# A hybrid decoder trunk on one core: the first sums of w2's quarters are queued on VectorE behind the last step of the layer norm ahead of the MLP

## The chip, the core and the metric

The kernel runs on one core of a Trainium2 chip. A core has TensorE (PE, matrix products into PSUM), VectorE (DVE), ScalarE (ACT) and GpSimd (POOL), each with an instruction queue of its own that is issued in order, and SyncE (SP), which here only issues transfers from the chip's main memory. Engines wait for each other by semaphores. The metric is the device time of one execution in microseconds. Three runs of the kernel before took 1161.6, 1162.25 and 1165.01 us; the median is 1162.25 us.

## The reference

Two decoder layers on 512 tokens of width 1024, in float32. Each layer is a token mixer and then an MLP, both with a residual and a layer norm behind them:

```python
for i in range(DEPTH):
    h = mixer_sb_ssm(x, ...) if i % 2 == 0 else mixer_dsa(x, ...)
    x = layer_norm(ALPHA * x + h, ln_mix_g[i], ln_mix_b[i])
    x = layer_norm(ALPHA * x + sq_relu_mlp(x, mlp_w1[i], mlp_w2[i]), ln_ffn_g[i], ln_ffn_b[i])

def sq_relu_mlp(x, w1, w2):
    return jnp.square(jax.nn.relu(x @ w1)) @ w2
```

Layer 0 mixes with stick-breaking attention beside a state-space model, layer 1 with sparse attention. w1 is 1024 x 4096, w2 4096 x 1024. This case is about the seam between mixer and MLP: the norm with `ln_mix`, and the first products with w1 and w2 behind it. It is passed twice, once in each layer.

## The kernel before

**Split products.** TensorE works on pairs: each float32 operand is split into a high part, rounded to a shorter format, and the low rest, and a product is three matmuls, high by high, high by low and low by high (`mm3`, lines 131 to 133; lines 841 to 843 in the mixers' projections; lines 311 to 313 in the products with w2). For a weight, ScalarE makes the high part (line 104, or 298 for quarters of w2) and VectorE or GpSimd the low one (line 105, or 299).

**The mixer's last projection.** `out_block` computes one block of 128 tokens by 512 columns in a PSUM bank and VectorE adds it to x (line 848, or line 846 for the first one). Token blocks are numbered 0 to 3 here.

**The layer norm.** When a token block's columns are complete, `layer_norm` runs: the statistics (`bn_stats`, line 181, and line 182), the variance plus a small constant (line 183), its power of -1/2 on GpSimd (line 184), two passes over the whole block with two inputs from SBUF (line 185 and line 189), then eight transposes on TensorE into two PSUM banks (line 199), whose high part ScalarE writes (line 202) and whose low part VectorE writes (line 203), into `xhi` and `xlo`. The MLP's first products read these.

**The MLP.** `up_raw` makes h in groups: `proj_halves` runs the first four column tiles of w1 for tokens 0 to 255 and then for 256 to 511, so that they can begin before the last norms. `down_chunk` multiplies 1024 rows of w2 with a scheme that saves products by forming sums of quarters: w2's chunk has the quarters b11, b12, b21 and b22, each in two tiles of 128 x 1024. It loads b11 and b12, and the first sum is

```python
b12 = load("b12", 0, 1)
combine(b12, b12, b11, ALU.subtract)
```

that is, `b12 - b11` in two instructions on VectorE (line 293), whose result is needed by the scheme's second product. A chunk is a third of w2's first 3072 rows; the first chunk of each MLP is the one with `r0 == 0`. Its loads can start early, since nothing else holds those buffers.

**What sets the order.** Nothing here is ordered by hand apart from the places that say so: a scheduler simulates the program and gives each engine the instruction that it takes to be ready first. An instruction that depends only on loads can so stand between the norms' steps. `issue_after(ins)` makes every instruction that is written inside its block stand behind `ins` on the engine of `ins`. It sets an order of issue only; there is no wait on `ins`.

Of the kernel before, what the change touches and what calls it, by code (L numbers as in the profile page):

```python
# [8 lines left out]
F32 = mybir.dt.float32  # L9
F32R = mybir.dt.float32r  # L10
AF = mybir.ActivationFunctionType
ALU = mybir.AluOpType
# [23 lines left out]
class Trunk:  # L36
# [135 lines left out]
    def layer_norm(self, t, gb, last):  # L172

        nc = self.nc
        xt = self.x[:, t, :]
        n = 2 if not last or t < NB - 1 else 4
        st = self.lnp.tile([P, n, 6], F32, tag="st", bufs=2, name=self.nm("st"))
        mv = self.lnp.tile([P, 2], F32, tag="mv", bufs=2, name=self.nm("mv"))
        rs = self.lnp.tile([P, 2], F32, tag="rs", bufs=2, name=self.nm("rs"))
        for h in range(n):  # L180
            nc.vector.bn_stats(st[:, h, :], xt[:, h * D // n:(h + 1) * D // n])
        nc.vector.bn_aggr(mv, st)
        nc.vector.tensor_scalar(rs[:, 0:1], mv[:, 1:2], LN_EPS, None, ALU.add)  # L183
        nc.gpsimd.tensor_tensor(rs[:, 1:2], rs[:, 0:1], self.mhalf, ALU.pow)  # L184
        nc.vector.scalar_tensor_tensor(xt, xt, mv[:, 0:1], gb[:, 0, :], ALU.subtract, ALU.mult)
        n = n // 2
        for h in range(n):
            c = slice(h * D // n, (h + 1) * D // n)
            nc.vector.scalar_tensor_tensor(xt[:, c], xt[:, c], rs[:, 1:2], gb[:, 1, c], ALU.mult, ALU.add)
            if last:  # L190
                (nc.scalar if h else nc.sync).dma_start(self.out[t * P:(t + 1) * P, c], xt[:, c])
        if last:
            return
        tok = slice(t * P, (t + 1) * P)
        for h in range(2):
            ps = self.bank("pst")
            for i in range(4):
                k = 4 * h + i
                nc.tensor.transpose(ps[:, i * P:(i + 1) * P], xt[:, k * P:(k + 1) * P], self.ident)
            pv = ps.rearrange("p (k c) -> p k c", c=P)  # L200
            hi = self.xhi[:, 4 * h:4 * h + 4, tok]
            nc.scalar.copy(hi, pv)  # L202
            nc.vector.tensor_tensor(self.xlo[:, 4 * h:4 * h + 4, tok], pv, hi.bitcast(F32), ALU.subtract)  # L203

    def mlp(self, w1, w2, g, b, last):

# [66 lines left out]
    def down_chunk(self, hp, w2, r0, hs, u, touched, last):  # L273

        nc, mm = self.nc, self.nc.tensor.matmul
        vec, act = nc.vector, nc.scalar
        a11, a21 = hs[0][:, :, 0:256], hs[0][:, :, 256:512]
        a12, a22 = hs[1][:, :, 0:256], hs[1][:, :, 256:512]  # L280

        def load(tag, j, n):
            ts = []
            for i in range(2):
                t = hp.tile([P, 1024], F32, tag=tag, bufs=2, name=self.nm(tag)).rearrange("p (k c) -> p k c", c=512)
                r = r0 + j * 512 + i * 256
                nc.sync.dma_start(t, w2[r:r + 256, n * 512:n * 512 + 512].rearrange("(k p) c -> p k c", p=P))
                ts.append(t)
            return ts

        def combine(out, x, y, op):
            for o, p, q in zip(out, x, y):
                vec.tensor_tensor(o, p, q, op)  # L293

        def halves(src, pool, c):
            hi = pool.tile([P, 1024], F32R, tag="whi", bufs=4, name=self.nm("whi")).rearrange("p (k c) -> p k c", c=c)
            lo = pool.tile([P, 1024], F32R, tag="wlo", bufs=4, name=self.nm("wlo")).rearrange("p (k c) -> p k c", c=c)
            act.copy(hi, src)  # L298
            vec.tensor_tensor(lo, src, hi.bitcast(F32), ALU.subtract)  # L299
            return hi, lo  # L300

        def product(a, b):
            pss = [self.psb.tile([P, 512], F32, tag="psb", name=self.nm("psb")) for _ in range(2)]
            ahi, alo = halves(a, self.wp, 256)
            for i in range(2):
                bhi, blo = halves(b[i], hp, 512)
                for t, ps in enumerate(pss):
                    tok = slice(t * P, (t + 1) * P)
                    for k in range(2):
                        lh, ll = ahi[:, 2 * i + k, tok], alo[:, 2 * i + k, tok]  # L310
                        mm(ps, lh, bhi[:, k, :], start=i + k == 0, stop=False)  # L311
                        mm(ps, lh, blo[:, k, :], start=False, stop=False)  # L312
                        mm(ps, ll, bhi[:, k, :], start=False, stop=i + k == 2)  # L313
            return pss

        def add(pss, row, col, op=ALU.add):
            for t, ps in enumerate(pss):
                xs = self.x[:, 2 * row + t, col * 512:col * 512 + 512]
                if (row, col, t) in touched:
                    vec.tensor_tensor(xs, xs, ps, op)  # L320
                else:
                    touched.add((row, col, t))
                    vec.scalar_tensor_tensor(xs, xs, ALPHA, ps, ALU.mult, op)

        def gather(pss):
            for t, ps in enumerate(pss):
                if ("u", t) not in touched:
                    touched.add(("u", t))
                    act.copy(u[:, t, :], ps)
                else:  # L330
                    vec.tensor_tensor(u[:, t, :], u[:, t, :], ps, ALU.add)

        b11 = load("b11", 0, 0)
        ps = product(a11, b11)
        add(ps, 0, 0)
        gather(ps)
        yield
        b12 = load("b12", 0, 1)
        combine(b12, b12, b11, ALU.subtract)
        vec.tensor_tensor(a21, a21, a22, ALU.add)  # L340
        ps = product(a21, b12)
        add(ps, 1, 1)
        add(ps, 0, 1)
        yield
        b22 = load("b22", 1, 1)
        vec.tensor_tensor(a11, a21, a11, ALU.subtract)
        s4 = hp.tile([P, 4, 256], F32, tag="s4", bufs=1, name=self.nm("s4"))
        vec.tensor_tensor(s4, a12, a11, ALU.subtract)
        add(product(s4, b22), 0, 1)
        yield  # L350
        combine(b12, b22, b12, ALU.subtract)
        b21 = load("b21", 1, 0)
        gather(product(a11, b12))
        yield
        vec.tensor_tensor(a11, a22, a11, ALU.subtract)
        combine(b11, b12, b11, ALU.subtract)
        ps = product(a11, b11)
        add(ps, 1, 0)
        add(ps, 1, 1)
        yield  # L360
        combine(b22, b12, b21, ALU.subtract)
        add(product(a12, b21), 0, 0)
        yield
        add(product(a22, b22), 1, 0, ALU.subtract)
        if last:
            for row, col in ((0, 1), (1, 0), (1, 1)):
                xs = self.x[:, 2 * row:2 * row + 2, col * 512:col * 512 + 512]
                vec.tensor_tensor(xs, xs, u, ALU.add)
        yield
# [838 lines left out]
```

## Time and profile before

| what | value |
|---|---|
| median of three runs | 1162.25 us |
| profiled execution, its own time | 1163.17 us |
| its span (first to last instruction) | 1161.4 us |
| mean granted TensorE clock | 0.987 |
| TensorE busy | 1111.9 us, 96% |
| VectorE busy | 840.6 us, 72% |
| ScalarE busy | 532.6 us, 46% |
| GpSimd busy | 172.2 us, 15% |
| line 293, all 48 instructions | 60.3 us on VectorE |

All times in a trace are microseconds from the span's start. A timeline row gives start, duration, engine, line, operation, output <- inputs, the tile's shape and how many equal instructions were merged; in brackets stand the engine's idle time before the row and what ended it. Durations of neighbours on an engine can overlap a little. In tile names numbers are left out, so `b` stands for any quarter of w2, `psb` for a PSUM bank of a projection, `pst` for one of transposes. A row of stretches gives for each stretch its length, the busy time and the instructions of TensorE, its weight loads, VectorE, ScalarE and GpSimd, then the granted clock of TensorE (1.00 is full speed), the share of the transfer engines and GB/s. The chain of waits is the work that ended last, followed back from the end; "issue" in it is time in which an engine waited for nothing that is seen.

The norm ahead of the MLP lies at 229 to 268 us in layer 0 and at 800 to 832 us in layer 1.

### The profile page before, as it was taken

To read this page: it belongs to the slowest core of one execution; us is meant where nothing else is said; L and a number is where in the kernel's file an instruction comes from. 1 tells how busy PE (TensorE), PEld (TensorE's weight loads), DVE (VectorE), ACT (ScalarE), POOL (GpSimd) and SP (SyncE) were. 2 spreads that over 40 slices of the span, in tenths; PEclk is the share of its full clock that TensorE was granted. 3 is DMA by queue.
4 is the path that set the end of the run, shared out by engine and by line. 5 is a ranking of instruction groups with operands and counts; after the bars stand their busy time and mean duration, and the time that the engine had idled before them with its cause. 6 is when DMAs were issued, how large, how long until landed. Compare 5 with 4: busy or idle time off the path is not lost.

```text
span 1161.4 us, 15563 instructions
## 1 busy us (share of the span) xinstructions
PE 1111.9 (96%) x5860; PEld 926.4 (80%) x5860; DVE 840.6 (72%) x1255; ACT 532.6 (46%) x832; POOL 172.2 (15%) x201
## 2 busy tenths in 40 slices
PE   7989999999999999999999979997999999999997
PEld 6878877779888888888898867775988888888886
DVE  7996598694667875965568998557548678587736
ACT  5534386424544444554135446552445445445520
POOL 1043230320000000000121655325000000000001
PEclk9998999999999999999999989998999999999999
DMA  7526683651243252333046860008304415315101
GB/s 246 143 62 157 189 223 96 194 168 39 61 145 101 62 159 73 97 112 87 1 120 158 216 189 1 2 9 264 109 19 127 131 33 152 120 38 162 37 1 73
DMA packets 147307, 126.99 MB, mean 109 GB/s; under 512 B 24353, under 2 KB 115297, under 8 KB 147233
## 3 DMA queue, kind: packets, MB, share of 16 engines
q1 hardware_dynamic: 145552, 123.59, 36.9%
q10 hardware_dynamic: 1680, 2.41, 0.6%
q8 instruction: 46, 0.75, 0.3%
q14 instruction: 29, 0.23, 0.1%
HBM read 105.80 MB, written 5.37 MB: 96 GB/s over the span
## 4 chain that ended last, share of the span: by engine, by line
PE 85%; DVE 6%; DMA 4%; issue 2%; ACT 2%; SPq 1%; POOL 0%; POOLq 0%; DVEq 0%; ACTq 0%
PE psa L131 12%; PE psa L133 12%; PE psa L132 12%; PE psb L311 7%; PE psb L313 7%; PE psb L312 7%; PE pso L949 3%; PE pst L942 3%; PE psb L382 3%; PE psb L381 3%; PE psb L380 3%; PE psl L1142 2%; PE psb L841 2%; PE psb L842 2%; PE psb L843 2%
## 5 line engine op out<-in xcount | busy, mean ns | idle before, releaser
L133 PE MATMUL psa<-xhi,wlo 128*128 128x512 f32 (+1 forms) x720 | 267.0, 371 | 0.0
L132 PE MATMUL psa<-xlo,whi 128*128 128x512 f32 (+1 forms) x720 | 266.5, 371 | 0.0
L131 PE MATMUL psa<-xhi,whi 128*128 128x512 f32 (+1 forms) x720 | 265.6, 371 | 0.2 <-ACT xhi L202 0.2
L104 ACT CAST whi<-raw 128x1024 fp32r<-128x1024 f32 (+1 forms) x129 | 133.6, 1046 | 204.6 <-PE psa L132 126.4
L105 DVE TENSOR_TENSOR wlo<-raw,whi 128x1024 fp32r<-128x1024 f32 (+1 forms) x102 | 128.2, 1260 | 86.9 <-ACT whi L104 85.8
L132 PEld LDWEIGHTS psa<-xlo,whi 128*128 128x128 f32 x720 | 135.7, 188 | 23.3 <-DVE xlo L203 0.4
L133 PEld LDWEIGHTS psa<-xhi,wlo 128*128 128x128 f32 x720 | 135.7, 188 | 23.2
L131 PEld LDWEIGHTS psa<-xhi,whi 128*128 128x128 f32 x720 | 135.0, 188 | 23.1 <-ACT xhi L202 0.5
L299 DVE TENSOR_TENSOR wlo<-b,whi 128x1024 fp32r<-128x1024 f32 x84 | 102.6, 1222 | 42.9 <-ACT whi L298 42.8
L311 PE MATMUL psb<-whi,whi 128*128 128x512 f32 x336 | 130.7, 389 | 0.0
L312 PE MATMUL psb<-wlo,whi 128*128 128x512 f32 x336 | 130.7, 389 | 0.0
L313 PE MATMUL psb<-whi,wlo 128*128 128x512 f32 x336 | 129.7, 389 | 0.0
L298 ACT CAST whi<-b 128x1024 fp32r<-128x1024 f32 x84 | 88.3, 1051 | 41.9 <-PE psb L313 30.2
L105 POOL TENSOR_TENSOR wlo<-raw,whi 128x1024 fp32r<-128x1024 f32 x27 | 69.7, 2591 | 135.6 <-ACT whi L104 134.5
L184 POOL TENSOR_TENSOR rs<-rs,two 128x1 f32<-128x1 f32 x16 | 22.4, 1402 | 424.2 <-DVE rs L183 424.2
L313 PEld LDWEIGHTS psb<-whi,wlo 128*128 128x128 f32 x336 | 63.1, 188 | 13.2
L312 PEld LDWEIGHTS psb<-wlo,whi 128*128 128x128 f32 x336 | 63.1, 188 | 13.1
L311 PEld LDWEIGHTS psb<-whi,whi 128*128 128x128 f32 x336 | 63.1, 188 | 13.0
L293 DVE TENSOR_TENSOR b<-b,b 128x1024 f32<-128x1024 f32 x48 | 60.3, 1262 | 12.3 <-DMA b<-in_w_dram 11.8
L298 ACT CAST whi<-h 128x1024 fp32r<-128x1024 f32 x36 | 38.0, 1054 | 54.0 <-PE psb L312 34.0
L299 DVE TENSOR_TENSOR wlo<-h,whi 128x1024 fp32r<-128x1024 f32 x36 | 44.0, 1222 | 14.2 <-ACT whi L298 13.5
L841 PE MATMUL psb<-whi,xhi 128*128 128x512 f32 x128 | 51.6, 411 | 0.8 <-DVE rs L183 0.6
(263 smaller groups left out, 1967.5 us busy)
## 6 DMA issues: line engine op xcount, KB each, us to landing
raw<-in_w_dram SPq DMA_DIRECT2D x80, 512.0 KB, 4.1
b<-in_w_dram SPq DMA_DIRECT2D x48, 512.0 KB, 4.6
raw<-in_w_in_dram SPq DMA_DIRECT2D x29, 512.0 KB, 4.4
raw<-in_w_out_dram SPq DMA_DIRECT2D x16, 512.0 KB, 4.6
qst<-hl SPq DMA_DIRECT2D x48, 128.0 KB, 3.5
kst<-hl SPq DMA_DIRECT2D x24, 256.0 KB, 4.4
gb<-in_ln_g_dram SPq DMA_DIRECT2D x4, 512.0 KB, 4.0
gb<-in_ln_b_dram SPq DMA_DIRECT2D x4, 512.0 KB, 5.2
```

Source lines behind the costliest of these rows:

```text
L104: nc.scalar.copy(hi[:, c], raw[:, c])
L105: (eng or nc.vector).tensor_tensor(lo[:, c], raw[:, c], hi[:, c].bitcast(F32), ALU.subtract)
L131: mm(ps, lhi, rhi, start=start, stop=False)
L132: mm(ps, lhi, rlo, start=False, stop=False)
L133: mm(ps, llo, rhi, start=False, stop=stop)
L293: vec.tensor_tensor(o, p, q, op)
L298: act.copy(hi, src)
L299: vec.tensor_tensor(lo, src, hi.bitcast(F32), ALU.subtract)
L311: mm(ps, lh, bhi[:, k, :], start=i + k == 0, stop=False)
L312: mm(ps, lh, blo[:, k, :], start=False, stop=False)
L313: mm(ps, ll, bhi[:, k, :], start=False, stop=i + k == 2)
L841: nc.tensor.matmul(ps, chi[:, k, tok], whi, start=i == 0, stop=False)
```

## The change

The last `tensor_tensor` that `layer_norm` writes (line 203, block 3's second half) is kept in `self.normed`, and the first chunk's first sum is written inside `issue_after(self.normed)`:

```diff
@@ layer_norm
-            nc.vector.tensor_tensor(self.xlo[:, 4 * h:4 * h + 4, tok], pv, hi.bitcast(F32), ALU.subtract)
+            last_lo = nc.vector.tensor_tensor(self.xlo[:, 4 * h:4 * h + 4, tok], pv, hi.bitcast(F32), ALU.subtract)
+        self.normed = last_lo.ins
@@ down_chunk
         b12 = load("b12", 0, 1)
-        combine(b12, b12, b11, ALU.subtract)
+        with self.tc.issue_after(self.normed) if r0 == 0 else nullcontext():
+            combine(b12, b12, b11, ALU.subtract)
         vec.tensor_tensor(a21, a21, a22, ALU.add)
```

Two instructions of each layer are so held behind the norm on VectorE; the loads, the other chunks and the arithmetic are the same. In the changed file lines move down by one from line 204 and by two from line 341: line 293 becomes 294, 299 becomes 300, 846 and 848 become 848 and 850.

Since the scheduler simulates the whole program, other instructions near the two places change their order too. On VectorE in layer 0, before (`x<-x,psb` adds a projection's half block; `psb_2262` is block 1's first half, `rs_2320` block 0's factor, `rs_2372` block 1's):

```order
L181 BN_STATS st_2318<-x 128x6
L293 TENSOR_TENSOR b_488_2898<-b_488_2898,b_472_2817 128x1024
L182 BN_AGGR mv_2319<-st_2318 128x2
L293 TENSOR_TENSOR b_489_2900<-b_489_2900,b_473_2819 128x1024
L848 TENSOR_TENSOR x<-x,psb_2262 128x512
L183 TENSOR_SCALAR rs_2320<-mv_2319 128x1
L185 SCALAR_TENSOR_TENSOR x<-x,mv_2319,gb_1311 128x1024
```

And now:

```order
L182 BN_AGGR mv_2319<-st_2318 128x2
L183 TENSOR_SCALAR rs_2320<-mv_2319 128x1
L185 SCALAR_TENSOR_TENSOR x<-x,mv_2319,gb_1311 128x1024
L850 TENSOR_TENSOR x<-x,psb_2262 128x512
L189 SCALAR_TENSOR_TENSOR x<-x,rs_2320,gb_1311 128x1024
L181 BN_STATS st_2370<-x 128x6
L850 TENSOR_TENSOR x<-x,psb_2276 128x512
L181 BN_STATS st_2370<-x 128x6
L182 BN_AGGR mv_2371<-st_2370 128x2
L183 TENSOR_SCALAR rs_2372<-mv_2371 128x1
L185 SCALAR_TENSOR_TENSOR x<-x,mv_2371,gb_1311 128x1024
L850 TENSOR_TENSOR x<-x,psb_2290 128x512
```

Block 0's steps now follow each other, and the sums stand 40 instructions later, between the last line 203 and the first line 300:

```order
L203 TENSOR_TENSOR xlo<-pst_2435,xhi 128x4x128
L294 TENSOR_TENSOR b_488_2898<-b_488_2898,b_472_2817 128x1024
L294 TENSOR_TENSOR b_489_2900<-b_489_2900,b_473_2819 128x1024
L300 TENSOR_TENSOR wlo_2828<-b_472_2817,whi_2827 128x1024
L300 TENSOR_TENSOR wlo_2844<-b_473_2819,whi_2843 128x1024
```

On TensorE in layer 0, block 0's transposes (`pst_2328`, `pst_2335`) stood behind both halves of block 2's projection, together with block 1's; now they stand between these halves, and block 1's first four behind the second half. Block 1's second four move behind the first matmul of the MLP, and block 2's eight stand together behind the first half of the MLP's matmuls for tokens 0 to 255; this half reads only what block 1's first four deliver, or `xhi`. In layer 1 TensorE's order is as it was. There VectorE had, before (`psb_7111`, `psb_7137` and `psb_7163` are blocks 0, 1 and 2):

```order
L293 TENSOR_TENSOR b_1367_7761<-b_1367_7761,b_1351_7680 128x1024
L293 TENSOR_TENSOR b_1368_7763<-b_1368_7763,b_1352_7682 128x1024
L846 SCALAR_TENSOR_TENSOR x<-x,psb_7111 128x512
L846 SCALAR_TENSOR_TENSOR x<-x,psb_7137 128x512
L181 BN_STATS st_7189<-x 128x6
L181 BN_STATS st_7239<-x 128x6
L846 SCALAR_TENSOR_TENSOR x<-x,psb_7163 128x512
```

And now, up to block 0's line 189:

```order
L848 SCALAR_TENSOR_TENSOR x<-x,psb_7111 128x512
L181 BN_STATS st_7189<-x 128x6
L848 SCALAR_TENSOR_TENSOR x<-x,psb_7137 128x512
L182 BN_AGGR mv_7190<-st_7189 128x2
L181 BN_STATS st_7239<-x 128x6
L848 SCALAR_TENSOR_TENSOR x<-x,psb_7163 128x512
L183 TENSOR_SCALAR rs_7191<-mv_7190 128x1
L185 SCALAR_TENSOR_TENSOR x<-x,mv_7190,gb_7084 128x1024
L181 BN_STATS st_7263<-x 128x6
L182 BN_AGGR mv_7240<-st_7239 128x2
L181 BN_STATS st_7263<-x 128x6
L189 SCALAR_TENSOR_TENSOR x<-x,rs_7191,gb_7084 128x1024
```

Block 0's line 189 now stands ahead of block 1's lines 183 and 185, and the two sums stand behind the last line 203 here too.

## The prediction, as put on record before the run

> **What bounds the kernel now.** I read the page first (share of the chain that ended last by engine), then TensorE's rows with an idle time, then the same stretches in the chain of waits and in VectorE's timeline.
>
> The page's part 4:
>
> ```profile
> PE 85%; DVE 6%; DMA 4%; issue 2%; ACT 2%; SPq 1%; POOL 0%; POOLq 0%; DVEq 0%; ACTq 0%
> ```
>
> TensorE is the path for 85% of 1161.4 us. An edit of VectorE's order pays only where TensorE waits for VectorE. TensorE's timeline around the two layer norms ahead of an MLP (start, duration, line; idle time before, releaser in brackets):
>
> ```profile
> 236.63 0.50 PE L841 MATMUL psb<-whi,xhi 128*128 128x512 f32 x1 [0.64 <-DVE rs L183]
> 245.23 1.23 PE L199 MATMUL pst<-ident,x 128*128 128x128 f32 x8 [1.99 <-DVE x L189]
> 265.59 1.03 PE L199 MATMUL pst<-ident,x 128*128 128x128 f32 x8
> ...
> 798.34 0.39 PE L843 MATMUL psb<-whi,xlo 128*128 128x512 f32 x1
> 800.61 0.39 PE L843 MATMUL psb<-whi,xlo 128*128 128x512 f32 x1
> 809.26 1.97 PE L199 MATMUL pst<-ident,x 128*128 128x128 f32 x8 [8.26 <-DVE x L189]
> 819.65 0.38 PE L132 MATMUL psa<-xlo,whi 128*128 128x256 f32 x1
> ```
>
> Layer 0 has two waits there (0.64 and 1.99 us), layer 1 one of 8.26 us, each for VectorE. The granted clock around layer 0's second wait (view by stretches; the number before the DMA share is the clock):
>
> ```profile
> 242.00:245.20 3.20, 1.25 (x10) 0.92 (x8) 3.20 (x6) 1.07 (x2) 1.53 (x1) 1.00 0.00 0
> 245.20:249.30 4.10, 4.07 (x16) 3.39 (x17) 4.07 (x8) 1.40 (x3) 0.69 (x1) 0.60 0.00 0
> 249.30:253.20 3.90, 3.90 (x18) 3.25 (x17) 3.43 (x5) 2.91 (x3) 0.77 (x1) 0.98 0.11 27
> ```
>
> After it the clock is 0.60 for 4.10 us, so 4.10 x 0.40 = 1.64 us more are lost. That the moved sums (line 293) stand in what TensorE waits for, the chain of waits shows:
>
> ```profile
> 231.92 1.30 DVE b L293
> 233.22 1.48 issue
> 234.69 0.20 DVE mv L182
> 234.89 1.09 DVE b L293
> ...
> 790.00 7.66 DMA b<-in_w_dram
> 797.78 1.30 DVE b L293
> 799.28 1.21 DVE b L293
> 800.50 1.19 DVE x L846 x2
> ```
>
> In layer 1 the chain even runs over the load of the quarter that the sum needs. VectorE's timeline:
>
> ```profile
> 231.92 2.85 DVE L293 TENSOR_TENSOR b<-b,b 128x1024 f32<-128x1024 f32 x1
> 234.81 1.17 DVE L293 TENSOR_TENSOR b<-b,b 128x1024 f32<-128x1024 f32 x1
> 236.56 1.27 DVE L185 SCALAR_TENSOR_TENSOR x<-x,mv,gb 128x1024 f32<-128x1024 f32 x1
> 243.90 1.28 DVE L189 SCALAR_TENSOR_TENSOR x<-x,rs,gb 128x1024 f32<-128x1024 f32 x1
> 272.96 1.22 DVE L299 TENSOR_TENSOR wlo<-b,whi 128x1024 fp32r<-128x1024 f32 x1 [4.83 <-ACT whi L298]
> ...
> 797.78 2.72 DVE L293 TENSOR_TENSOR b<-b,b 128x1024 f32<-128x1024 f32 x2 [1.76 <-DMA b<-in_w_dram]
> 800.42 1.27 DVE L846 SCALAR_TENSOR_TENSOR x<-x,psb 128x512 f32<-128x512 f32 x2
> 814.46 3.95 DVE L105 TENSOR_TENSOR wlo<-raw,whi 128x1024 fp32r<-128x1024 f32 x3 [0.17 <-ACT whi L104]
> 818.92 1.28 DVE L203 TENSOR_TENSOR xlo<-pst,xhi 128x512 fp32r<-128x512 f32 x2
> 836.34 1.23 DVE L299 TENSOR_TENSOR wlo<-b,whi 128x1024 fp32r<-128x1024 f32 x1 [4.93 <-ACT whi L298]
> ```
>
> The sums hold VectorE 2.85 + 1.17 = 4.02 us in layer 0 and 2.72 us in layer 1 (after 1.76 us of waiting). At the place they move to, behind the last line 203 and ahead of the first line 299, VectorE sits idle for 4.83 and 4.93 us.
>
> **The change part by part.** Nothing is added or removed: four sums, two in each layer, change their place on VectorE; no DMA moves, and SyncE's and GpSimd's orders are the same. In layer 0 TensorE's order and one cast of ScalarE change too.
>
> *Layer 0.* With the sums gone, token block 0's norm starts at 231.92, where the first sum started. Its mean (line 182) and line 183 end by about 232.2; the two-input pass of line 185 comes next. GpSimd is still splitting weights then:
>
> ```profile
> 225.49 8.20 POOL L105 TENSOR_TENSOR wlo<-raw,whi 128x1024 fp32r<-128x1024 f32 x3 [0.87 <-ACT whi L104]
> 236.72 1.53 POOL L184 TENSOR_TENSOR rs<-rs,two 128x1 f32<-128x1 f32 x1 [3.03 <-DVE rs L183]
> ```
>
> It ends at 233.69, and the sum that ran beside it took 2.85 us, its sister 1.17. So line 185 costs between 1.27 and 2.85 us; I take the slow end, because GpSimd's work lies under it: done by about 234.9. Line 184 cannot start before 233.7 and takes 1.53, so line 189 has its factor at 235.3. Behind line 185 stands line 848 for block 1's first half (0.6 us: the two of line 846 at 800.42 take 1.27), done by 235.5. It frees the PSUM bank that TensorE waited for until 236.63; the matmuls before that wait ended at 236.63 - 0.64 = 235.99. **The 0.64 us go.** Line 189 then ends at about 236.7.
>
> TensorE now runs block 2's first half of the projection (12 matmuls of 0.227 us: from 798.34 to 800.61 there are ten) from about 235.8 to 238.55 and then block 0's transposes, which the new order puts there: ready since 236.7. Block 2's second half fills 239.6 to 242.3, and the transposes of block 1 follow. They need the second line 189, which before ended at 243.90 + 1.28 = 245.18. From 236.7 VectorE has ahead of it lines 181, 848, 181, 182, 183, 185, 848 and 189, 0.6 + 0.6 + 0.6 + 0.2 + 0.1 + 1.2 + 0.6 + 1.2 = 5.1 us, so 241.8. **TensorE arrives at 242.3: the 1.99 us go**, with 0.5 us to spare, and I let the slow clock of 1.64 us go with the gap. Layer 0: 0.64 + 1.99 + 1.64 = **4.3 us**. As a check I count what TensorE issues from 235.8 to the transposes of block 3 without a wait: 48 matmuls of the projection x 0.227, 96 of the MLP's first half x 0.12 (six in 0.72 us below), six fours of transposes x 0.5 (1.03 us for eight), 10.9 + 11.5 + 3.0 = 25.4: 261.2 in place of 265.59, 4.4 us. Block 3's line 189 follows block 2's transposes by a cast, a split, lines 182 to 185 and line 184 on GpSimd, and I put it at 260.6, some 0.5 us before.
>
> ```profile
> 820.11 0.28 PE L132 MATMUL psa<-xlo,whi 128*128 128x256 f32 x1
> ...
> 820.83 0.28 PE L132 MATMUL psa<-xlo,whi 128*128 128x256 f32 x1
> ```
>
> *Layer 1.* Here the sums waited for their load. The matmul at 798.34 ends block 0's projection (0.39 later, 798.73); VectorE can take line 846 at 798.77 and not at 800.42: **1.65 us**. From there to the splits of block 1 (818.92) VectorE runs the same set of instructions in both orders, with one wait of 0.17 us in 18.5, so the splits come 1.65 to 1.8 us earlier; I take **1.7**. Line 189 of block 0 rises over other blocks' passes: from 798.77 it has 7.0 us of passes to its end (seven of 0.6, two means, line 183, two of 1.2), 805.8 in place of 809.1. TensorE's 8.26 us shrink by 3.3 to about 5; but at 819.65 it needs block 1's splits, which three weight splits (3.95 us) hold up, and there it waits out the difference, about 1.6 us. Bounds: 1.65 (VectorE all the way) and 3.3 (if TensorE alone counted).
>
> *At the new place* the sums cost 2 x 1.2 = 2.4 us, in idle times of 4.83 and 4.93. Queued behind them is line 299 of the unsummed quarter, which waits for ScalarE anyway. The summed quarter's cast comes later:
>
> ```profile
> 276.08 1.05 ACT L298 CAST whi<-b 128x1024 fp32r<-128x1024 f32 x1 [0.17 <-issue]
> ```
>
> With everything 4.3 us earlier it comes at 271.8, the first sum ends near 265: nothing is late. Without that cover it would be 2.4 us in each layer.
>
> **Sum:** 4.3 + 1.7 = 6.0 us. Behind both places TensorE is busy (no idle time over 0.4 us from 270 to 600 and from 810 on), and weight loads start when buffers come free, so the gain should be kept. The profiled execution took 1163.17 (1.8 around its span): 1157.2. It lies 0.9 above the median of 1162.25, from which it would be 1156.2. I say **1157**.
>
> [...] The row first: a gap of 1.99 us was followed by a clock of 0.60. [...]
>
> ```profile
> 611.66 0.59 PE L1084 MATMUL psx<-kist,qist 96*128 96x256 f32 x3 [1.76 <-issue]
> 611.60:616.00 4.40, 4.34 (x35) 4.21 (x36) 2.80 (x6) 1.97 (x7) 0.00 (x0) 1.00 1.06 268
> ```
>
> [...]
>
> **The rivals.** (1) *The slow clock stays.* The gap goes, but the work from 245 on meets a clock of 0.60 for 4.1 us all the same. For it: 1.76 us did not slow TensorE at 611.66. Against: the slow stretch begins with the first transposes behind the gap. Gain 4.4: 1158.8.
>
> (2) *The wait moves on.* My spare time in layer 0 is 0.5 us at blocks 1 and 3. If VectorE's chain comes 2 us late at one of them, TensorE waits there, and the clock falls again: 4.3 - 2.0 - 1.6 = 0.7, with layer 1's 1.7 a gain of 2.4: 1160.8. For it: GpSimd's overlap, and a queue now packed with norm passes. Against: 5.1 us of passes counted row by row.
>
> (3) *Nothing arrives.* A load behind these places sets the pace, and both gains are waited out there: 1163.2. For it: in layer 1 the chain ran through a load of w2. Against: DMA is 4% of the chain, and that load leaves it.
>
> (4) *Slower: the sums hold up the MLP.* They go from a stretch in which TensorE still waits for other things to the head of the products. If the cast at 276.08 waited for them and the norms gained nothing, 2 x 2.4 = 4.8 us: 1168.0. It decides once the sums end later than that cast could start, over 6 us later than I have them. Against: the idle 4.83 and 4.93 us.
>
> **How the numbers follow.** Forecast 0.60, rivals 0.11, 0.11, 0.11 and 0.07. A measurement of this kernel can tell about 0.3%, 3.5 us, from no change. The forecast is faster by that, the first rival nearly always; (2) and (3) are within it: faster 0.70, same 0.23, slower 0.07. The range: below, layer 1's bound of 3.3 with the lower median, 1162.25 - 7.6 = 1154.6, and a us for runs; above, the second rival with its scatter: 1153.5 to 1161.5. Left out are most of (3) and (4).
>
> **What would show it.** In the changed trace: no idle time of TensorE over 0.4 us and a clock of 1.00 from 236 to 253; the transposes of block 3 near 261.1; line 846 near 798.8; TensorE's gap in layer 1 near 5 us and a second one of 1 to 2 us ahead of the first line 132; line 294 inside VectorE's idle time ahead of line 300. Wrong would be: a gap at the transposes of block 1 or 3 of layer 0, or a time above 1159.

## The result and the profile after

| what | before | changed kernel |
|---|---|---|
| median of six runs | 1164.26 us (1161.6 to 1165.01) | 1156.85 us (1155.07 to 1158.38) |
| ratio of the times, 95% interval | | 0.9946 (0.9934 to 0.9959) |
| profiled execution, its own time | 1163.17 us | 1157.72 us |
| its span | 1161.4 us | 1155.9 us |

The change makes the kernel 0.54% faster, between 0.41 and 0.66%. The two medians lie 7.4 us or 0.64% apart, still inside that interval. Forecast were 1157 us and a gain of 6.0 us; the gain is 5.45 us between the two profiled executions and, by the ratio, 6.3 us. Of the page's shares of the chain that ended last, this is the row by engine; TensorE's share was 85% before, the transfers' (DMA) 4%:

```profile
PE 86%; DVE 7%; DMA 3%; issue 2%; ACT 1%; SPq 1%; POOL 0%; POOLq 0%; DVEq 0%; ACTq 0%
```

TensorE's timeline of the changed kernel around the two norms (lines of the changed file, so 199 is as before, 843 to 845 are the projection's products):

```profile
239.41 1.04 PE L199 MATMUL pst<-ident,x 128*128 128x128 f32 x8
243.04 0.60 PE L199 MATMUL pst<-ident,x 128*128 128x128 f32 x4
261.79 1.04 PE L199 MATMUL pst<-ident,x 128*128 128x128 f32 x8
...
802.87 1.97 PE L199 MATMUL pst<-ident,x 128*128 128x128 f32 x8 [4.86 <-DVE rs L183]
813.64 0.66 PE L199 MATMUL pst<-ident,x 128*128 128x128 f32 x4 [0.33 <-DVE x L848]
814.24 0.39 PE L132 MATMUL psa<-xlo,whi 128*128 128x256 f32 x1
```

In layer 0 no transpose waits any more. In layer 1 the long wait is 4.86 us instead of 8.26. (The view names line 183 as what ended it; block 0's line 189, which these transposes read, ended beside it, at 802.81.) The view by stretches says the same of layer 0 (length; busy time of TensorE, its weight loads, VectorE, ScalarE, GpSimd; granted clock): TensorE is busy for all of 26 us and its clock is 1.00 throughout.

```profile
236.00:262.00 26.00, 26.00 (x174) 23.82 (x173) 24.29 (x35) 7.55 (x10) 4.47 (x4) 1.00 0.48 146
```

VectorE's timeline of the changed kernel at the places that the prediction costed:

```profile
229.83 0.68 DVE L850 TENSOR_TENSOR x<-x,psb 128x512 f32<-128x512 f32 x1
233.19 2.42 DVE L185 SCALAR_TENSOR_TENSOR x<-x,mv,gb 128x1024 f32<-128x1024 f32 x1
236.14 1.27 DVE L189 SCALAR_TENSOR_TENSOR x<-x,rs,gb 128x1024 f32<-128x1024 f32 x1
241.47 1.28 DVE L189 SCALAR_TENSOR_TENSOR x<-x,rs,gb 128x1024 f32<-128x1024 f32 x1
259.97 1.28 DVE L189 SCALAR_TENSOR_TENSOR x<-x,rs,gb 128x1024 f32<-128x1024 f32 x1 [0.44 <-POOL rs L184]
264.25 2.35 DVE L294 TENSOR_TENSOR b<-b,b 128x1024 f32<-128x1024 f32 x2
269.18 1.23 DVE L300 TENSOR_TENSOR wlo<-b,whi 128x1024 fp32r<-128x1024 f32 x1 [2.58 <-ACT whi L299]
...
795.78 0.69 DVE L848 SCALAR_TENSOR_TENSOR x<-x,psb 128x512 f32<-128x512 f32 x1 [2.49 <-PE psb L845]
809.49 3.49 DVE L105 TENSOR_TENSOR wlo<-raw,whi 128x1024 fp32r<-128x1024 f32 x3
813.50 1.88 DVE L203 TENSOR_TENSOR xlo<-pst,xhi 128x512 fp32r<-128x512 f32 x3
825.91 2.35 DVE L294 TENSOR_TENSOR b<-b,b 128x1024 f32<-128x1024 f32 x2
830.92 1.23 DVE L300 TENSOR_TENSOR wlo<-b,whi 128x1024 fp32r<-128x1024 f32 x1 [2.65 <-ACT whi L299]
```

The sums stand in what was idle time: ahead of the first line 300 VectorE is now idle for 2.58 and 2.65 us, and before for 4.83 and 4.93. Within 0.1 us that is the sums' 2.35 us: they took up idle time.

**Where the 5.5 us of span come from.** I cut both executions at the same five places. The first is the start of the first add of the projection (before: the row below; after: 229.83). The second is the transposes of block 3 in layer 0 (265.59, 261.79). The third is the end of TensorE's work ahead of its long wait in layer 1 (809.26 - 8.26 = 801.00; 802.87 - 4.86 = 798.01). The fourth is the first line 132 of layer 1 (819.65, 814.24). The last is the end. The row of the kernel before, from VectorE's timeline:

```profile
228.99 0.67 DVE L848 TENSOR_TENSOR x<-x,psb 128x512 f32<-128x512 f32 x1
```

| stretch | before | after | difference |
|---|---|---|---|
| start to the first add | 228.99 | 229.83 | +0.84 |
| to the transposes of block 3, layer 0 | 36.60 | 31.96 | -4.64 |
| to the long wait of layer 1 | 535.41 | 536.22 | +0.81 |
| to the first line 132 of layer 1 | 18.65 | 16.23 | -2.42 |
| to the end | 341.75 | 341.66 | -0.09 |

The two norms gave 4.64 and 2.42 us, 7.06 together. 1.65 us of it were lost in stretches that the edit doesn't touch. Of the first loss (0.84 us), 0.54 us are there within the first 12 us: a matmul that starts at 11.35 us before starts at 11.89 us now. Of the second (0.81 us), 0.69 us come with the clock. TensorE's timeline shows the attention's products of layer 1 behind a long wait that both kernels have (of the same length, though the view names another end for it); of the kernel before:

```profile
692.35 5.57 PE L1142 MATMUL psl<-kst,qst 128*128 128x384 f32 x24 [7.11 <-DVE pst L1149]
```

and of the changed kernel:

```profile
688.68 6.26 PE L1144 MATMUL psl<-kst,qst 128*128 128x384 f32 x24 [7.10 <-DMA qst<-hl]
```

They are the same 24 products, and they take 0.69 us longer. The granted clock from their start on was 0.66 over 6.3 us before and 0.55 over 6.4 us after. Why that differs between two executions of equal work, no run here shows; the last section comes back to it.

### The profile page after: what moved, and what is told of

Its sections match the earlier page's. It is cut to its first block, busy times and chain, and to the rows that moved or that the text cites. A ratio compares the mean times of both kernels' runs of the same rounds, so it can differ in the third digit from the quotient of the medians.

```text
span 1155.9 us, 15562 instructions
## 1 busy us (share of the span) xinstructions
PE 1113.2 (96%) x5860; PEld 928.3 (80%) x5860; DVE 839.0 (73%) x1255; ACT 532.8 (46%) x832; POOL 172.4 (15%) x201
## 4 chain that ended last, share of the span: by engine, by line
PE 86%; DVE 7%; DMA 3%; issue 2%; ACT 1%; SPq 1%; POOL 0%; POOLq 0%; DVEq 0%; ACTq 0%
PE psa L132 12%; PE psa L133 12%; PE psa L131 12%; PE psb L313 7%; PE psb L314 7%; PE psb L312 7%; PE pso L951 3%; PE pst L944 3%; PE psb L383 3%; PE psb L382 3%; PE psb L384 3%; PE psb L843 2%; PE psl L1144 2%; PE psb L844 2%; PE psb L845 2%
```

## The experiments

Each edit is made to the changed kernel, and each median stands beside runs of the kernel before on the same chip.

**One layer at a time.** The sums are held in layer 0 alone:

```diff
-        with self.tc.issue_after(self.normed) if r0 == 0 else nullcontext():
+        with self.tc.issue_after(self.normed) if r0 == 0 and self.n_mlp == 1 else nullcontext():
```

> Only layer 0's first sums are held behind the norm; layer 1 stays as before. My theory (VectorE's passes ahead of the transposes are the price, and the slow clock goes with the gap): 4.3 to 4.7 us under the kernel before, ratio about 0.996; no idle time of TensorE over 0.4 us and a clock of 1.00 at 236 to 262 us of the span, layer 1's gap 8 us as before. Rival (the slow clock is not the gap's and stays): 2.6 to 3 us under before, with a clock near 0.6 for some 4 us near 245.

Measured: 1160.5 us against 1164.43, ratio 0.9964 (0.9952 to 0.9976), so 4.2 us less. Its TensorE has no idle time from 236 to 253 us and a clock of 1.00; in layer 1 its wait is like that of the kernel before:

```profile
236.00:253.00 17.00, 17.00 (x99) 14.84 (x98) 16.86 (x26) 6.47 (x8) 2.98 (x2) 1.00 0.44 143
...
806.61 1.97 PE L199 MATMUL pst<-ident,x 128*128 128x128 f32 x8 [8.46 <-DVE x L189]
```

In layer 1 alone (`self.n_mlp == 2` in the same place):

> Only layer 1's first sums are held; layer 0 stays as before. My theory: 1.7 to 2.4 us under the kernel before, ratio 0.998 to 0.9985: the gap shrinks from 8.3 to about 4.9 us, but VectorE's splits of block 1 set the pace behind it. Layer 0 shows its gap of 2 us and the slow clock behind it once more; the two single changes add up to the whole, 6 to 7 us. Rival (TensorE's gap counts in full): 3.4 us under before, ratio 0.997.

Measured: 1161.01 us against 1164.43, ratio 0.9971 (0.9962 to 0.9981), so 3.4 us less, with an interval of 2.2 to 4.4. The interval takes in my 2.4 and the rival's 3.4. From its trace:

```profile
246.18 1.09 PE L199 MATMUL pst<-ident,x 128*128 128x128 f32 x8 [1.97 <-DVE x L189]
...
806.75 1.97 PE L199 MATMUL pst<-ident,x 128*128 128x128 f32 x8 [4.85 <-DVE x L189]
818.12 0.38 PE L132 MATMUL psa<-xlo,whi 128*128 128x256 f32 x1
```

From the end of the projection (806.75 - 4.85 = 801.90) to the first line 132 it takes 16.22 us, 2.4 less than before (18.65) and 3.0 less than with layer 0 alone (there from 806.61 - 8.46 = 798.15 to 817.40: 19.25). So layer 1 is worth 2.4 to 3.0 us. In this execution layer 0's wait of 1.97 us was there, but the eight transposes behind it took 1.09 us and not 1.23, and the granted clock over the 4.1 us from them on was 1.00: no slow clock followed it. The two layers' ratios take 0.36 and 0.29% off, 0.65 together; the whole change takes 0.54% (0.41 to 0.66). Within that noise they add up.

**How much room the new place has.** The held sums are undone and made again once (so six sums stand where two would do), and then three times:

```diff
             combine(b12, b12, b11, ALU.subtract)
+            for _ in range(1 if r0 == 0 else 0):
+                combine(b12, b12, b11, ALU.add)
+                combine(b12, b12, b11, ALU.subtract)
```

> The change, with the held sum made three times in each layer's first chunk (b12 - b11, + b11, - b11; the result is the same but for rounding): 4 more instructions of 1.2 us in each layer at the new place. My theory: they fill VectorE's idle time there (2.6 us up to the first line 300, then 0.2, 1.5 and more) and end before the summed quarter's cast, so the time stays within 1 us of the changed kernel, ratio to before about 0.994. Rival (the sums hold up the MLP's products): 4.8 us in each layer more, 9.6 in all, ratio about 1.002.

Measured: 1156.9 us, ratio 0.9939 (0.9925 to 0.9952): no cost, as expected.

> The change, with the held sum made seven times: 12 more instructions, 14 us in each layer, at the new place. They end some 9 us behind the place where the summed quarter's cast stands in the changed kernel, and the splits of the unsummed quarter are late too. My theory: here the cover is gone; each layer loses something between 2 and 9 us, the time lies 4 to 18 us above the changed kernel. Rival (nothing waits for VectorE there, since the first products come much later): within 1.5 us of the changed kernel.

Measured: 1156.16 us, ratio 0.9936 (0.9923 to 0.9949). Twelve sums more, some 14 us of VectorE in each layer, cost nothing, and my expectation of 4 to 18 us fell. VectorE's and ScalarE's rows of that run:

```profile
263.69 5.76 DVE L294 TENSOR_TENSOR b<-b,b 128x1024 f32<-128x1024 f32 x5
273.91 6.89 DVE L294 TENSOR_TENSOR b<-b,b 128x1024 f32<-128x1024 f32 x6
283.38 1.06 ACT L299 CAST whi<-b 128x1024 fp32r<-128x1024 f32 x1 [0.39 <-DVE b L294]
297.64 1.23 DVE L345 TENSOR_TENSOR h<-h,h 128x1024 f32<-128x1024 f32 x1 [6.27 <-ACT h L229]
```

The scheduler laid line 300's splits between the sums and moved the summed quarter's cast back; that cast waits 0.39 us for a sum, and VectorE still idles for 6.27 us ahead of 297.64. So the cover at the new place isn't the 4.8 us of one idle time but the idle times of VectorE behind it taken together. The fourth rival's price (2.4 us a layer, from a delay of 6 us on) has no place here: 14 us didn't reach it.

**One sum held, one left free.**

```diff
-            combine(b12, b12, b11, ALU.subtract)
+            combine(b12[:1], b12[:1], b11[:1], ALU.subtract)
+        combine(b12[1:], b12[1:], b11[1:], ALU.subtract)
```

> The change with only the first of the two sums held behind the norm in each layer; the second is free, and the scheduler puts it behind block 0's line 185 in layer 0 and ahead of block 0's projection sum in layer 1, and TensorE's order in layer 0 differs from the change's. Theory (each sum of 1.2 us on VectorE ahead of the transposes counts about once, less the spare time of 0.5 us and the wait for the load): 1 to 2.5 us above the changed kernel, ratio to before 0.995 to 0.997. Rival (only the first sum, the one of 2.85 us beside GpSimd, was the cost): within 0.7 us of the changed kernel.

Measured: 1164.84 us against 1165.02, ratio 1.000 (0.9991 to 1.001). Nothing is left of the gain; my theory and its rival both had some. TensorE and VectorE:

```profile
253.37 0.58 PE L132 MATMUL psa<-xlo,whi 128*128 128x256 f32 x1 [2.62 <-DVE xlo L203]
...
801.43 1.22 DVE L294 TENSOR_TENSOR b<-b,b 128x1024 f32<-128x1024 f32 x1 [2.62 <-DMA b<-in_w_dram]
...
811.42 1.97 PE L199 MATMUL pst<-ident,x 128*128 128x128 f32 x8 [7.86 <-DVE x L189]
```

In layer 1 the reason is plain: the free sum still waits for its load in front of the norm, so VectorE stands for 2.62 us, and TensorE waits 7.86. In layer 0 block 1's transposes went behind block 3's projection in TensorE's order, and the wait moved on to the first line 132: 2.62 us, and a clock of 0.50 from 253.37 up to 259.1. That is the prediction's second rival, seen in a neighbour of the change. One free sum, with the other order that the scheduler then gave both engines, was enough for it. So the runs show what the held sums and the new order do together; none of them shows what the 4.02 us of VectorE's time alone would have given in layer 0.

**Is TensorE short of cover in layer 1?** I let the scheduler write each norm of layer 1 three blocks behind its projection and not two, so that another projection stands in front of block 0's transposes:

```diff
-                                   for t in range(NB)], gb, False)
+                                   for t in range(NB)], gb, False, 3)
```

> The change, and in layer 1's mixer the norms follow three blocks behind the projection and not two, so that TensorE has block 3's 24 matmuls (5.4 us) in the gap of 4.9 us that the change leaves there. VectorE's order keeps the three weight splits of line 105 ahead of block 1's splits. Theory (VectorE is the bound of layer 1's seam): the gap closes and opens again at the first lines 199 or 132, the time stays within 1 us of the changed kernel, ratio about 0.994. Rival (TensorE's gap and the slow clock behind it are the cost): 4 to 6 us under the changed kernel, ratio about 0.990.

Measured: 1160.64 us against 1164.26, ratio 0.9969 (0.9958 to 0.9981). That is 2.7 us more than the changed kernel by the ratios, whose intervals just touch (0.9958 and 0.9959); I had expected a change of a us at most, the rival a gain. Both were wrong about the time. Its TensorE:

```profile
802.83 1.09 PE L199 MATMUL pst<-ident,x 128*128 128x128 f32 x8 [0.55 <-DVE rs L183]
808.81 1.97 PE L199 MATMUL pst<-ident,x 128*128 128x128 f32 x8 [4.90 <-DVE x L189]
813.59 0.39 PE L132 MATMUL psa<-xlo,whi 128*128 128x256 f32 x1 [1.77 <-DVE xlo L203]
```

The wait of 4.9 us closes at block 0 (0.55) and opens again at block 1 (4.90). VectorE had, between block 0's line 189 and block 1's, two weight splits that depend on a load and its cast alone (of its timeline):

```profile
804.55 1.21 DVE L105 TENSOR_TENSOR wlo<-raw,whi 128x1024 fp32r<-128x1024 f32 x1
805.79 1.17 DVE L105 TENSOR_TENSOR wlo<-raw,whi 128x1024 fp32r<-128x1024 f32 x1
807.48 1.28 DVE L189 SCALAR_TENSOR_TENSOR x<-x,rs,gb 128x1024 f32<-128x1024 f32 x1
```

It is the sums' fault again with other instructions. So the splits alone were held behind block 1's norm:

```diff
@@ layer_norm
+        if t == 1:
+            self.normed_1 = last_lo.ins
@@ up_raw
-                        ps = self.proj_fm(w1, (c * 8 + f) * P, None)
+                        with self.tc.issue_after(self.normed_1) if first and self.n_mlp == 2 else nullcontext():
+                            ps = self.proj_fm(w1, (c * 8 + f) * P, None)
```

> The change, and in layer 1 the low parts of w1's next four column tiles (line 105) are queued behind block 1's last split on VectorE. Theory: VectorE's chain to block 1's splits is 3.5 us shorter, but TensorE, still with its gap of 4.9 us and the slow clock, arrives only 0.3 to 0.6 us before the splits of the changed kernel: 0.3 to 1 us under the changed kernel, ratio about 0.9938. Rival (VectorE alone is the bound): 3.5 us under it, ratio 0.9915.

Measured: 1158.13 us, ratio 0.9948 (0.9935 to 0.996), as the changed kernel; the rival's 3.5 us fall, and the 0.3 to 1 us of my theory can't be told from nothing. TensorE still waits for block 0's norm, and VectorE then waits for TensorE, where the splits stood:

```profile
803.47 1.82 PE L199 MATMUL pst<-ident,x 128*128 128x128 f32 x8 [4.85 <-DVE rs L183]
...
811.71 0.69 DVE L851 SCALAR_TENSOR_TENSOR x<-x,psb 128x512 f32<-128x512 f32 x1 [1.53 <-PE psb L848]
```

Then both edits together:

> Both edits of the two runs before. Theory (each of two chains of about the same length sets the pace, so only both together pay): 2.5 to 4.5 us under the changed kernel, ratio 0.990 to 0.992, with 1 to 3 us of waiting left ahead of block 1's transposes or first line 132. Rival (a third thing sets the pace, such as the power on GpSimd or the casts): within 1 us of the changed kernel.

Measured: 1154.47 us (1152.79 to 1155.91), ratio 0.9916 (0.9902 to 0.9931), as expected: faster than both kernels, by 3.5 us against the change by the ratios, and the intervals do not touch. TensorE's waits there are 2.25 and 1.58 us, and eight transposes take 1.09 us, at a granted clock of 1.00 (801.29 to 811.52):

```profile
805.62 1.09 PE L199 MATMUL pst<-ident,x 128*128 128x128 f32 x8 [2.25 <-DVE x L189]
809.26 0.39 PE L132 MATMUL psa<-xlo,whi 128*128 128x256 f32 x1 [1.58 <-DVE xlo L203]
```

Either edit alone gives nothing or costs; the later norms need a VectorE that is free for them, and the free VectorE needs work of TensorE that comes first.

**Three more executions** were to show whether the slow clock behind layer 0's wait is a rule. The kernel before, twice, and layer 1 alone, once more:

> The kernel before, profiled once more. The gap of 2.0 us in layer 0 left a clock of 0.60 for 4.1 us in the first profile and a clock of 1.00 in the run with layer 1's change alone. If the slow clock follows such a gap by chance, this profile shows either; if the first was the rule it shows 0.6 again. The time is 1161 to 1167 us.

> The kernel before, profiled a third time, for the clock behind layer 0's gap of 2.0 us. So far 0.60, 0.65 and, with layer 1's change, 1.00 over the 4.1 us from the transposes on. If it is chance, either may show; if layer 1's change made the difference, it is near 0.6 again.

> Layer 1's change alone, profiled again, for the same clock. Chance: either 1.00 or about 0.6. If layer 0 of this kernel differed in something, 1.00 again, though its order there is that of the kernel before.

They took 1163.47, 1167.35 and 1162.34 us, one execution each. All three had the wait ahead of layer 0's transposes (1.97, 1.99 and 1.95 us) and a slow clock behind it (0.64, 0.67 and 0.61 over 4.1 us). The last section sets them beside the execution without it.

## Why the prediction was right, point by point

- **Layer 0: 4.3 us forecast, 4.64 measured** (4.2 by the runs with layer 0 alone). All three terms went: the 0.64 us at the PSUM bank, the 1.99 us at the transposes, and the slow clock, for which the clock of 1.00 over 26 us stands. Block 3's transposes come 31.96 us behind the first add; I had put them at 261.1 to 261.2, and without the 0.84 us by which this execution came later to the norm they are at 260.95.
- **Its working held in detail.** Line 185 beside GpSimd (three weight splits there, 226.32 to 234.53) took 2.42 us (bounds 1.27 and 2.85, taken 2.85). Without the 0.84 us, block 0's line 189 ends at 236.57 (237.41 in the row; 236.7 forecast), the second one at 241.9 (242.75; 241.8 forecast), and TensorE's transposes for it begin at 242.2 (243.04; 242.3 forecast): a spare of 0.3 us where I had 0.5. The second rival's danger was real, as the run with one sum held shows.
- **Layer 1: 1.7 us forecast, 2.42 measured: the term was mis-sized.** VectorE's head start was right: line 848 starts as soon as TensorE's first block ends, which gives 1.65 us. Its start, 795.78, is the forecast 798.77 less the 2.99 us by which the changed kernel was ahead by then, and the chain that ended last now comes to it from TensorE's last product of that block, and no longer over a load. Wrong was "VectorE runs the same set of instructions in both orders, with one wait of 0.17 us in 18.5". From the first line 848 to the splits of block 1 it now takes 813.50 - 795.78 = 17.72 us. Of the 0.78 us, 0.17 are the wait and 0.46 the three weight splits, 3.49 us now and 3.95 before: the merged row hid pauses for ScalarE's casts. The rest, 0.15 us, I can't place. ScalarE's timeline has the third of these casts, before:

```profile
816.09 1.06 ACT L104 CAST whi<-raw 128x1024 fp32r<-128x1024 f32 x1 [0.30 <-PE psb L843]
```

and in the changed kernel:

```profile
810.13 1.06 ACT L104 CAST whi<-raw 128x1024 fp32r<-128x1024 f32 x1 [0.32 <-PE psb L845]
```

Before, it ended at 817.15 and the third split, some 1.2 us long, followed it at once, up to 818.4. Now it ends at 811.19, and VectorE comes to the third split at about 811.8. The casts wait for TensorE's work on block 3, which came 6.0 us earlier, while VectorE's splits came 5.0 us earlier (814.46, 809.49). So a queue that I took as VectorE's alone ran partly at TensorE's pace, and TensorE gained more.
- **The second wait of layer 1, 1.6 us forecast ahead of line 132, was 0.33**, at the transposes just ahead of it. TensorE's long wait shrank by 3.4 us (3.3 forecast, to about 5). From its end to the first line 132 TensorE took 10.39 us before (809.26 to 819.65) and 11.37 now (802.87 to 814.24). So it waited out 0.98 us in place of 1.6, since VectorE was faster. Of these, 0.33 show as a wait; about 0.4 went into a slow clock that lasted 0.8 us longer behind the long wait (the clock is 0.50 up to 807.11, 4.24 us behind that wait; before, up to 812.67, 3.41 us), and the rest is below what I can place.
- **The new place: free, as forecast**, but for a smaller reason than there was. I had covered 2.4 us by an idle time of 4.8; there was room for 16 us at least.
- **The sum.** The terms gave 6.0 us and the norms 7.06. The profiled execution kept 5.5 us of span, since 0.84 us ahead of the norms and 0.81 us between the layers went the other way. That 1157 met 1156.85 so closely is in part luck, these errors against each other. By the ratio the gain is 6.3 us (4.8 to 7.7).
- **The rivals.** The slow clock did not stay (rival 1). The wait did not move on (2) in the change, though it does with one sum. The gain arrived (3): 341.75 and 341.66 us behind layer 1's norm. No sum held up the MLP (4).

## What to carry to other kernels

Where a scheduler issues what is ready first, an instruction that depends on a load alone can stand inside a chain of short dependent steps for which the busiest engine waits; look for it in that engine's wait rows and in the chain of waits, and move all such instructions, since one that stays can keep the whole cost. Before moving them, look how far behind the new place the first reader is, and not only at the next idle time. If a later norm or a free engine helps only together with the other, test the two as a pair.

## What was not expected of the hardware

**The same wait of about 2 us was followed by a slow clock in four profiles and not in the fifth.** Layer 0's wait ahead of its transposes stands in five profiles: the kernel before three times (1.99, 1.97 and 1.99 us) and layer 1 alone twice (1.97 and 1.95 us). In the first of them the granted clock is 0.50 from 246.06 to 249.47, 3.41 us, and 1.00 on both sides. Stretches of that length around the wait, in the kernel before (its profile of the start, then that of a later execution) and then with layer 1 alone (the execution without a slow clock), are these. The second number is TensorE's busy time in the stretch, the one ahead of the last two is its clock:

```profile
242.65:246.06 3.41, 1.42 (x14) 1.19 (x13) 3.41 (x5) 1.21 (x3) 1.15 (x1) 1.00 0.00 0
246.06:249.47 3.41, 3.41 (x11) 2.73 (x10) 3.38 (x7) 1.44 (x3) 0.85 (x1) 0.50 0.00 0
```

```profile
243.01:246.42 3.41, 1.44 (x13) 1.20 (x11) 3.41 (x6) 1.43 (x3) 0.88 (x1) 1.00 0.00 0
246.42:249.83 3.41, 3.41 (x9) 2.64 (x9) 3.30 (x7) 1.60 (x3) 1.13 (x1) 0.50 0.00 0
```

```profile
240.92:244.34 3.42, 3.29 (x19) 2.61 (x17) 3.42 (x8) 0.53 (x2) 1.12 (x1) 1.00 0.01 4
244.34:247.75 3.41, 1.57 (x11) 1.49 (x12) 3.41 (x5) 1.42 (x4) 0.41 (x1) 1.00 0.00 0
247.75:251.16 3.41, 3.41 (x16) 2.79 (x16) 3.38 (x7) 2.31 (x3) 1.46 (x1) 1.00 0.02 5
```

In the first two TensorE is busy for 1.42 and 1.44 us of the 3.41 with the wait, and the next stretch runs at 0.50. In the third the wait begins 0.13 us ahead of the stretch, which has 1.57 us of work, and the next stays at 1.00. The other two profiles with this wait had 1.42 and 1.46 us of work in such a stretch and a clock of 0.50 in the next. In the best version, with a wait of 2.25 us, two stretches have 2.07 and 1.83 us of work, and the clock stays at 1.00:

```profile
801.29:804.70 3.41, 2.07 (x14) 1.58 (x12) 3.41 (x7) 2.04 (x3) 1.53 (x1) 1.00 0.51 183
804.70:808.11 3.41, 1.83 (x12) 1.39 (x12) 3.41 (x6) 1.07 (x2) 1.15 (x1) 1.00 0.00 0
808.11:811.52 3.41, 2.26 (x18) 2.26 (x19) 3.41 (x5) 0.00 (x0) 0.31 (x1) 1.00 0.00 0
```

The busy time ahead doesn't tell which wait a slow clock follows. With one sum held, a stretch of layer 0 with 1.64 us of work (248.87 to 252.28, with the start of the wait of 2.62 us) was followed by a clock of 0.50, and in the attention of the changed kernel one with 2.01 us of work was too:

```profile
605.73:609.14 3.41, 2.01 (x16) 1.69 (x15) 2.06 (x3) 2.27 (x6) 0.00 (x0) 1.00 1.18 268
609.14:612.55 3.41, 3.41 (x18) 3.41 (x18) 1.79 (x4) 0.43 (x2) 0.00 (x0) 0.50 0.95 228
```

What made the one execution of five differ is not shown by these runs. A stretch of 3.41 us at 0.50 costs 1.7 us (an estimate: half of 3.41). In the attention the kernel before had a clock of 1.00 from 605 to 630 us in its first execution and of 0.93 in its third. The slow stretches around the end of the wait at 692 us (0.50 for 6.83 us before, from 689.79, and for 10.24 in the changed kernel, from 684.23) go with 0.69 of the 1.65 us by which the two profiled executions differ where the edit does nothing; the slow stretch at 609 us left no more than 0.14 us by the start of that wait. The prediction's 1.64 us for the slow clock was right for the execution that I had; on the average of many I estimate less, by four profiles of five some 1.3 us.

A wait of 1.76 us left the clock at 1.00 in the kernel before (611.66), which the prediction's first rival had for it. For layer 0's wait that is no measure: waits of 1.95 to 1.99 us were followed by a clock of 0.50 in four profiles of five.
